# First block of a two-model kernel: when the local attention of the last two token tiles is issued, and which PSUM banks it and the gates use

## The chip, the cores and the metric

The kernel runs on one core of one Trainium2 chip, as one launch. The metric is the device time of an execution in microseconds. Before the change the median of three runs was 1892.68 us, from 1889.23 to 1899.89.

## The reference, cut to what matters

512 tokens of width 1024 pass through a "first block" and then through a second model of two layers. Only the first block's mixer is touched. It projects the normed input and feeds three mixers whose outputs are concatenated and projected again:

```python
proj = h @ w_in
att = swa_sink_alibi(a_q, a_k, a_v, attn_sinks)       # local attention, 4 heads, sinks, ALiBi
ssd = ssd_mixer(s_z, s_xbc, s_dt, ...)                # state space mixer, gated by silu(s_z)
gdn = gdn_mixer(g_qkv, g_z, g_b, g_a, ...)            # gated delta rule, gated by silu(g_z)
mix = jnp.concatenate([att, ssd, gdn], axis=-1) @ w_out
```

The local attention of a token sees its own chunk of 64 tokens and the two before it. It depends on nothing but its queries, keys and values. The delta rule solves a triangular system inside each chunk (this gives u and w), and then carries a 64x64 state per head through the 8 chunks, one after the other. The state space mixer carries a state through the tokens as well.

## The kernel before, in words

All matrices are fp32. A large product is made of three products with operands split into a high and a low part (lines 366 to 368 with the weight stationary, `fm`; lines 380 to 382 with the activation stationary, `tm_k`). Weights come in by DMA on SP's queue, and ScalarE and VectorE split them (lines 345 and 346).

`block1_mix` works on four token tiles of 128 tokens (`t` from 0 to 3). In source order it makes: the norm and the first small projections; the projections with a short convolution (`conv`, `fm_block`); the chunk stage of the delta rule (`chunk_stage`) and a substitution on 16x16 blocks; then the part that the change touches:

- a first loop over the tiles that widens the inverse of the chunk's triangle (lines 808 to 818),
- `ssd(0)`, `swa(0)`, `ssd(1)`, `swa(1)`,
- a second loop over the tiles that gives `gU` and `gW` (lines 823 to 834),
- `ssd(2)`, `swa(2)`,
- a third loop that makes the chunk's transition matrices `At` (lines 838 to 862),
- `ssd(3)`, `swa(3)`,
- the recurrence over 8 chunks (lines 866 to 896): per chunk four matmuls on the state (line 883), a copy of half the result by VectorE (885) and half by ScalarE (886), and the outputs (890, 894),
- the gates: three projections with `k.tm` in 12 groups of 24 matmuls (lines 380 to 382), each group ending in a tanh on ScalarE (447) and a multiply on VectorE (448), which both read the group's PSUM bank,
- norms, transposes into the operand of the output projection (`put_group`, line 357), and the output projection `out_proj`. It takes its eight row blocks in the order `WO1 = (6, 7, 4, 5, 0, 1, 2, 3)`: attention first (6, 7), then the delta rule (4, 5), then the state space mixer.

`swa(t)` does one tile of local attention: for each of two pairs of heads, two matmuls (749), scores with the bias and their maximum (750), softmax on VectorE and ScalarE (753 to 762), four transposes (766, two for tile 0) and a copy (768); then `swa` multiplies with the values (774) and copies the result to `oT` (775). It takes a PSUM bank five times.

PSUM has eight banks. `k.rings` gives names to lists of banks, and `k.ps(name, ...)` hands out the next bank of that list in turn, in source order; whoever gets a bank waits until the last user of it has been read out.

Source order isn't the order on the engines. When the program is built, a planner puts the instructions of each engine in a fixed order: of those that it holds for ready by its own estimates, the one that stands first in the source goes first. So the gates' matmuls, which stand late in the source and need only the normed input and their weights, appear early in the trace between other work. On the chip each engine then keeps that order.

Of the kernel before, what the change touches and what calls it, by code (L numbers as in the profile page):

```python
# [409 lines left out]
def block1_mix(k):  # L410
# [9 lines left out]
    def tile_(shape, name, bufs=1, dt=F32):  # L420
        return (late if name in LATE else P).tile(shape, dt, name=name, bufs=bufs)
# [40 lines left out]
    def bc(ap, n):  # L462

        return ap.unsqueeze(len(ap.shape)).to_broadcast(list(ap.shape) + [n])
# [271 lines left out]
    def swa(t):  # L736
        n = 256 if t else 128
        nk = n // 128
        c0 = t * 128 - (n - 128)
        mx = tile_([128, 4, 4], "amx", 2)  # L740
        pTs = []
        for hp in range(2):
            hs = slice(2 * hp, 2 * hp + 2)
            q = slice(hp * 64, hp * 64 + 64)
            pl = k.ps("s" if t > 1 else "w", [128, 2, 256])
            pr = tile_([128, 2, 256], "cvy", 2)
            for i in range(2):
                h = 2 * hp + i
                E.matmul(pl[:, i, :n], qT[i][q, tok(t)], kT[q, c0:c0 + n], start=True, stop=True)
                V.tensor_tensor_reduce(pr[:, i, :n], pl[:, i, :n], ali[:, h, 256 - n:], scale=1.0,  # L750
                                       scalar=k.row("sinks")[:, h:h + 1], op0=ALU.add, op1=ALU.max,
                                       accum_out=mx[:, 0, h:h + 1])
            V.tensor_scalar(mx[:, 1, hs], mx[:, 0, hs], -1.0, None, op0=ALU.mult)
            V.tensor_tensor(mx[:, 2, hs], k.row("sinks")[:, hs], mx[:, 0, hs], op=ALU.subtract)
            S.activation(mx[:, 2, hs], mx[:, 2, hs], AF.Exp)
            for i in range(2):
                h = 2 * hp + i
                S.activation(pr[:, i, :n], pr[:, i, :n], AF.Exp, bias=mx[:, 1, h:h + 1], accum_out=mx[:, 3, h:h + 1])
            V.tensor_tensor(mx[:, 3, hs], mx[:, 3, hs], mx[:, 2, hs], op=ALU.add)
            V.reciprocal(mx[:, 3, hs], mx[:, 3, hs])  # L760
            for i in range(2):
                V.tensor_scalar(pr[:, i, :n], pr[:, i, :n], mx[:, 3, 2 * hp + i:2 * hp + i + 1], None, op0=ALU.mult)
            pp = k.ps("s" if t > 1 else "w", [128, nk, 2, 128])
            for j in range(nk):
                for i in range(2):
                    E.transpose(pp[:, j, i, :], pr[:, i, j * 128:j * 128 + 128], k.ident)
            pT = tile_([128, 2, 2, 128], "a2w", 2)
            S.copy(pT[:, :nk], pp)
            pTs.append(pT)
        po = k.ps("s" if t > 1 else "w", [128, 2, 128])  # L770
        for hp in range(2):
            q = slice(hp * 64, hp * 64 + 64)
            for j in range(nk):
                E.matmul(po[q], av[:, t - (nk - 1) + j, q], pTs[hp][:, j], start=(j == 0), stop=(j == nk - 1))
        S.copy(oT[:, :, tok(t)], po)

    k.rings(g=(0,1), d=(2, 3, 4), s=(5,6), w=(7,))

    gU = tile_([128, NT, 4, 64], "gU")
    gW = tile_([128, NT, 4, 64], "xt", 3)  # L780
# [2 lines left out]
    def off(t, m):  # L783
        g = tile_([128, 4, 128], "t2k", 5)
        V.tensor_tensor(g.rearrange("p h (c i) -> p h c i", c=2),
                        gA[:, t, :, None, :].to_broadcast([128, 4, 2, 64]),
                        k.c(m).rearrange("p (c i) -> p c i", c=2)[:, None].to_broadcast([128, 4, 2, 64]),
                        op=ALU.mult)
        return g

    def mm4(p, a, b, start=True, stop=True):
        for h in range(4):
            E.matmul(p[:, h, :], a[:, h, :], b(h), start=start and (stop or h == 0), stop=stop and (start or h == 3),
                     skip_group_check=not (start and stop))

    def t2(p):
        o = tile_([128, 4, 128], "t2k", 5)
        S.copy(o, p)
        return o
# [6 lines left out]
    for t in range(NT):  # L806
        d = Dt[t]
# [10 lines left out]
        V.tensor_tensor(d, d, p, op=ALU.add)  # L818
    ssd(0)
    swa(0)  # L820
    ssd(1)
    swa(1)
    for t in range(NT):
        d = Dt[t]
        g2 = off(t, "off32")
        pv = k.ps("d", [128, 4, 128])
        mm4(pv, d, lambda h: rhs[:, t, :, h * 64:h * 64 + 64], stop=False)
        v0 = t2(pv)
        pw = k.ps("d", [128, 4, 128])
        mm4(pw, g2, lambda h: v0[:, h, :])  # L830
        v1 = t2(pw)
        mm4(pv, d, lambda h: v1[:, h, :], start=False)
        V.tensor_tensor(gU[:, t], pv[:, :, 0:64], bc(beta[:, t, :], 64), op=ALU.mult)
        V.tensor_tensor(gW[:, t], pv[:, :, 64:128], bc(nbeta[:, t, :], 64), op=ALU.mult)
    ssd(2)
    swa(2)

    pair = lambda w, q, t, p: w[q, t, 2 * p:2 * p + 2, :].rearrange("p a d -> p (a d)")
    At = []
# [21 lines left out]
                    V.scalar_tensor_tensor(a[r, p, r], k.ident[r, r], sdec[r, t, p, c:c + 1], pa[r, p, r],  # L861
                                           op0=ALU.mult, op1=ALU.add)
    ssd(3)
    swa(3)

    st = [tile_([128, 2, 128], f"st{i}") for i in range(2)]
    for z in st:
# [2 lines left out]
    for t in range(NT):  # L870
        for c in range(2):
# [15 lines left out]
            if c == 0:  # L887
                po = k.ps("d", [128, 4, 64])
# [688 lines left out]
```

## Time and profile before

| | before |
|---|---|
| median of 3 runs | 1892.68 us (1889.23 to 1899.89) |
| profiled execution | 1889.21 us, of which the span from the first to the last instruction is 1887.4 us |
| busy in the span | TensorE 98%, VectorE 56%, ScalarE 39%, GpSimd 7% |
| mean granted clock of TensorE | 0.994 of full |

The profile page has one line per view; the trace can be asked for each engine's instructions in order of time. A row of that timeline gives start, duration, engine, source line, operation, output and inputs, and shape; instructions of one line that follow each other are merged, with their number behind the x. In square brackets stands the idle time of the engine before the row and what ended it. The end of a matmul is modelled and runs into the next one's start, so what a group of matmuls takes is read from its start to the next row's start.

### The profile page before, as it was taken

The page shows a single profiled execution, that of the slowest core. Times are in us where ns is not written, and L with a number is a line of the kernel's source. Part 1 is how long each engine was busy: PE and PEld are TensorE (multiplying, and loading weights), DVE is VectorE, ACT ScalarE, POOL GpSimd, SP SyncE. Part 2 cuts the span into 40 slices and gives each one's busy share as a digit, 9 for nine tenths or more (in the row PEclk, how much of TensorE's full clock was granted, in tenths as well). Part 3 has the DMA queues.
Part 4 walks back from the last instruction along what each step waited for, and adds up shares of the span by engine and source line. Part 5 has one row for each costly group of instructions (what it writes and reads, how often), then busy time and mean ns, then how long its engine had stood idle before and what let it go on. Part 6 is the DMA issues. An engine that isn't in the chain of part 4 may idle for free.

```text
span 1887.4 us, 24192 instructions
## 1 busy us (share of the span) xinstructions
PE 1840.8 (98%) x9467; PEld 1529.9 (81%) x9467; DVE 1066.4 (56%) x1998; ACT 728.2 (39%) x1258; POOL 127.0 (7%) x165
## 2 busy tenths in 40 slices
PE   6999999999999999998999999999999999999998
PEld 6889868888888888865678888888898888888886
DVE  7877776432233357972366643664775476525655
ACT  4533345332332235454644432442433254323432
POOL 1402300000000020121100000000010000000000
PEclk9999999999999999999999999999999999999999
DMA  5221024333333213311043333333333343233321
GB/s 174 79 74 45 23 68 166 102 101 87 103 100 95 74 46 108 107 46 45 22 160 123 93 87 112 92 92 95 96 102 89 101 126 99 90 100 101 95 73 45
DMA packets 49090, 171.50 MB, mean 91 GB/s; under 512 B 5912, under 2 KB 6320, under 8 KB 48720
## 3 DMA queue, kind: packets, MB, share of 16 engines
q1 hardware_dynamic: 44928, 157.90, 27.2%
q10 hardware_dynamic: 3168, 8.25, 1.4%
q0 software_dynamic: 880, 3.82, 0.6%
q8 instruction: 74, 1.21, 0.3%
q14 instruction: 40, 0.33, 0.1%
HBM read 167.81 MB, written 2.13 MB: 90 GB/s over the span
## 4 chain that ended last, share of the span: by engine, by line
PE 50%; ACT 1%; DVE 0%; issue 0%; ACTq 0%; DVEq 0%
PE bank L367 10%; PE bank L366 10%; PE bank L368 10%; PE bank L381 6%; PE bank L382 6%; PE bank L380 6%; PE bank L357 1%; ACT lg L1338 0%; PE bank L1359 0%; ACT pT L1347 0%; ACT whi L345 0%; PE bank L1503 0%; ACT acth L345 0%; PE bank L1366 0%; ACT tsq L984 0%
## 5 line engine op out<-in xcount | busy, mean ns | idle before, releaser
L346 DVE TENSOR_TENSOR wlo<-wraw,whi 128x1024 fp32r<-128x1024 f32 (+3 forms) x295 | 356.3, 1210 | 469.8 <-ACT whi L345 460.6
L366 PE MATMUL bank<-acth,whi 128*128 128x512 f32 (+1 forms) x1528 | 575.7, 379 | 4.7 <-ACT qk L1204 2.9
L367 PE MATMUL bank<-actl,whi 128*128 128x512 f32 (+1 forms) x1528 | 576.1, 378 | 1.9 <-DVE actl L346 1.9
L368 PE MATMUL bank<-acth,wlo 128*128 128x512 f32 (+1 forms) x1528 | 576.0, 377 | 0.0
L345 ACT CAST whi<-wraw 128x1024 fp32r<-128x1024 f32 (+3 forms) x295 | 303.7, 1032 | 590.6 <-PE bank L367 322.2
L366 PEld LDWEIGHTS bank<-acth,whi 128*128 128x128 f32 x1528 | 286.9, 189 | 60.2 <-ACT qk L1204 3.8
L367 PEld LDWEIGHTS bank<-actl,whi 128*128 128x128 f32 x1528 | 288.0, 189 | 54.5 <-DVE actl L346 2.7
L368 PEld LDWEIGHTS bank<-acth,wlo 128*128 128x128 f32 x1528 | 288.1, 189 | 52.2 <-issue 0.3
L380 PE MATMUL bank<-whi,acth 128*128 128x512 f32 (+3 forms) x896 | 317.4, 356 | 4.8 <-ACT v L1478 1.9
L381 PE MATMUL bank<-wlo,acth 128*128 128x512 f32 (+3 forms) x896 | 317.4, 354 | 0.0
L382 PE MATMUL bank<-whi,actl 128*128 128x512 f32 (+3 forms) x896 | 316.0, 354 | 0.0
L380 PEld LDWEIGHTS bank<-whi,acth 128*128 128x128 f32 x896 | 171.0, 191 | 31.2 <-ACT v L1478 2.2
L381 PEld LDWEIGHTS bank<-wlo,acth 128*128 128x128 f32 x896 | 171.4, 191 | 23.5 <-DVE wlo L346 0.5
L382 PEld LDWEIGHTS bank<-whi,actl 128*128 128x128 f32 x896 | 171.1, 191 | 22.7
L1118 DVE SCALAR_TENSOR_TENSOR cv<-bank,fcw,cv 128x510 f32<-128x510 f32 x88 | 65.7, 748 | 2.8
L1117 DVE SCALAR_TENSOR_TENSOR cv<-bank,fcw,cv 128x511 f32<-128x511 f32 x88 | 65.4, 744 | 0.0
L345 ACT CAST acth<-cv 128x512 fp32r<-128x512 f32 x48 | 29.8, 620 | 86.1 <-DVE cv L1135 86.1
L1134 ACT ACTIVATE cv<-cv 128x512 f32<-128x512 f32 x44 | 27.8, 632 | 86.4 <-DVE cv L1118 86.4
L1116 ACT ACTIVATE cv<-bank,fcw 128x512 f32<-128x512 f32 x88 | 59.9, 681 | 0.0
L1131 DVE TENSOR_TENSOR cv<-cv,bank 128x512 f32<-128x512 f32 x22 | 15.1, 688 | 73.8 <-PE bank L368 73.1
L382 PE MATMUL bank<-whi,hid 128*128 128x512 f32 x144 | 56.3, 391 | 0.0
L381 PE MATMUL bank<-wlo,hid 128*128 128x512 f32 x144 | 56.2, 390 | 0.0
(387 smaller groups left out, 1755.2 us busy)
## 6 DMA issues: line engine op xcount, KB each, us to landing
wraw<-in_wf_dram SPq DMA_DIRECT2D x192, 512.0 KB, 3.5
wraw<-in_w_dram SPq DMA_DIRECT2D x63, 512.0 KB, 3.6
wraw<-in_wo_dram SPq DMA_DIRECT2D x24, 512.0 KB, 3.7
gain<-in_gains_dram ACTq DMA_DIRECT2D x12, 512.0 KB, 4.4
wraw<-in_wf_dram SPq DMA_DIRECT2D x12, 256.0 KB, 2.6
xt<-in_x_dram SPq DMA_DIRECT2D x4, 512.0 KB, 5.4
x<-in_x_dram SPq DMA_DIRECT2D x4, 512.0 KB, 5.7
out_dram<-x SPq DMA_DIRECT2D x8, 256.0 KB, 2.0
```

What stands on the lines that cost most here:

```text
L345: self.nc.scalar.copy(hi, src)
L346: (eng or self.nc.vector).tensor_tensor(lo, src, hi.bitcast(F32), op=ALU.subtract)
L366: self.nc.tensor.matmul(ps[:, s], hi[:, k, :], ah, start=(k == 0), stop=False)
L367: self.nc.tensor.matmul(ps[:, s], hi[:, k, :], al, start=False, stop=False)
L368: self.nc.tensor.matmul(ps[:, s], lo[:, k, :], ah, start=False, stop=(k == nk - 1))
L380: self.nc.tensor.matmul(ps, ah, wh, start=first, stop=False)
L381: self.nc.tensor.matmul(ps, ah, wl, start=False, stop=False)
L382: self.nc.tensor.matmul(ps, al, wh, start=False, stop=last)
L1116: S.activation(o, ps, AF.Copy, scale=w(2))
L1117: V.scalar_tensor_tensor(o[:, 1:], ps[:, :T - 1], w(1), o[:, 1:], op0=ALU.mult, op1=ALU.add)
L1118: V.scalar_tensor_tensor(o[:, 2:], ps[:, :T - 2], w(0), o[:, 2:], op0=ALU.mult, op1=ALU.add)
L1134: S.activation(g, g, AF.Silu)
```

## The change

The change does three things. `swa` takes its banks from the ring "w" for every tile (before: "s" for tiles 2 and 3). The ring "w" gets bank 1 beside bank 7, and the ring "g" of the gates keeps bank 0 alone. `swa(2)` moves ahead of the second loop, and `swa(3)` to the place behind `ssd(2)` where `swa(2)` was, ahead of the third loop.

```diff
-            pl = k.ps("s" if t > 1 else "w", [128, 2, 256])
+            pl = k.ps("w", [128, 2, 256])
...
-            pp = k.ps("s" if t > 1 else "w", [128, nk, 2, 128])
+            pp = k.ps("w", [128, nk, 2, 128])
...
-        po = k.ps("s" if t > 1 else "w", [128, 2, 128])
+        po = k.ps("w", [128, 2, 128])
...
-    k.rings(g=(0,1), d=(2, 3, 4), s=(5,6), w=(7,))
+    k.rings(g=(0,), d=(2, 3, 4), s=(5, 6), w=(7, 1))
...
     swa(1)
+    swa(2)
     for t in range(NT):
...
     ssd(2)
-    swa(2)
+    swa(3)
...
     ssd(3)
-    swa(3)
```

## Rows read from the trace of the kernel before

**Rows 1.** Stretches: PE, PEld, DVE, ACT, POOL busy (instructions), granted clock, DMA share, GB/s.

```profile
149.30:266.40 117.10, 116.47 (x929) 101.19 (x927) 87.78 (x223) 46.85 (x121) 33.80 (x28) 1.00 0.11 33
266.40:279.87 13.47, 10.57 (x41) 5.80 (x40) 9.78 (x61) 6.70 (x21) 0.00 (x0) 0.75 0.39 129
215.00:247.00 32.00, 32.00 (x271) 26.62 (x270) 23.52 (x76) 12.36 (x37) 2.55 (x3) 1.00 0.08 21
```

**Rows 2.** Timeline of TensorE at the end of the mixer.

```profile
265.77 0.70 PE L749 MATMUL bank<-cw 64*128 64x256 f32 x2
266.40 0.65 PE L894 MATMUL bank<-st,qtT 128*64 128x128 f32 x4
267.05 0.70 PE L749 MATMUL bank<-cw 64*128 64x256 f32 x2
269.30 1.16 PE L749 MATMUL bank<-cw 64*128 64x256 f32 x2 [1.55 <-DVE amx L750]
...
279.87 0.50 PE L380 MATMUL bank<-whi,acth 128*128 128x512 f32 x1 [0.56 <-ACT acth L345]
```

**Rows 3.** The second stretch, lines 766, 774 and 357 alone: PE, PEld, clock, DMA.

```profile
266.40:279.87 13.47, 2.16 (x8) 1.40 (x8) 0.75 0.39 129
266.40:279.87 13.47, 3.05 (x8) 1.22 (x8) 0.75 0.39 129
266.40:279.87 13.47, 3.14 (x16) 2.04 (x16) 0.75 0.39 129
```

**Rows 4.** Timeline of TensorE: products at full clock, each with its successor.

```profile
237.77 1.08 PE L774 MATMUL bank<-a2w,av 128*64 128x256 f32 x4
238.78 0.37 PE L856 MATMUL bank<-ktil,xt 64*128 64x128 f32 x1
...
317.64 0.39 PE L380 MATMUL bank<-whi,acth 128*128 128x512 f32 x1
317.87 1.03 PE L357 MATMUL bank<-cst,ty 128*128 128x128 f32 x8
318.66 0.48 PE L381 MATMUL bank<-wlo,acth 128*128 128x512 f32 x1
```

**Rows 5.** Timeline of TensorE: last product of swa(2), start and last products of ssd(3).

```profile
244.95 1.08 PE L774 MATMUL bank<-a2w,av 128*64 128x256 f32 x4
245.96 0.44 PE L678 MATMUL bank<-cst,cv 128*128 128x128 f32 x2
...
258.99 1.10 PE L700 MATMUL bank<-xdt,a2k 128*128 128x64 f32 x8
```

**Rows 6.** Timelines of ScalarE and VectorE: last tile of the recurrence, copied and normed.

```profile
267.08 0.37 ACT L896 COPY gU<-bank 128x256 f32<-128x256 f32 x1 [1.81 <-PE bank L894]
275.89 0.43 DVE L918 TENSOR_TENSOR gU<-gU,ro 128x256 f32<-128x256 f32 x1
```

**Rows 7.** Timeline of VectorE: two steps of a reciprocal root in succession.

```profile
252.96 0.17 DVE L405 TENSOR_TENSOR nw<-nw 128x6 f32<-128x6 f32 x1
253.16 0.17 DVE L406 TENSOR_TENSOR nw<-nw,nw 128x6 f32<-128x6 f32 x1
```

**Rows 8.** Timelines of TensorE, VectorE and ScalarE: starts and read-outs of gate groups.

```profile
157.51 0.27 PE L380 MATMUL bank<-whi,acth 128*128 128x192 f32 x1
158.07 0.35 DVE L448 SCALAR_TENSOR_TENSOR gz<-gz,bank 128x192 f32<-128x192 f32 x1 [1.11 <-ACT gz L447]
...
164.98 0.30 PE L380 MATMUL bank<-whi,acth 128*128 128x256 f32 x1
167.05 0.35 DVE L448 SCALAR_TENSOR_TENSOR gz<-gz,bank 128x192 f32<-128x192 f32 x1
...
193.83 0.67 ACT L447 ACTIVATE xt<-bank 128x256 f32<-128x256 f32 x2
195.54 0.74 DVE L448 SCALAR_TENSOR_TENSOR xt<-xt,bank 128x256 f32<-128x256 f32 x2
```

**Rows 9.** A stretch, tile cvy (probabilities of swa(3)) alone: PE, PEld, DVE, ACT.

```profile
260.00:280.00 20.00, 2.16 (x8) 1.40 (x8) 3.07 (x8) 2.36 (x8) 0.83 0.27 89
```

## The prediction

> **What bounds the kernel now.** I read the stretches first. From 149.30 us, where the last convolution's matmuls end, to 266.40, where the recurrence's last four matmuls start, TensorE is busy for 116.47 of 117.10 us at full clock: in this part of the mixer it never waits for more than 0.63 us in all, because the gates' matmuls stand in wherever the chains pause [rows 1]. The next 13.47 us are another matter: VectorE and ScalarE are busy for 9.78 and 6.70 us, and TensorE's granted clock averages 0.75 of full, that is, a part at 1.2 GHz after the engine had idled [rows 1]. The timeline shows why. Behind the recurrence's last products (line 894) TensorE has left only attention (line 749, then 766 and 774), which waits for VectorE, and transposes (line 357), until the output projection starts at 279.87 [rows 2, 3]. After that TensorE is full again for the rest of the kernel (98% of the span). So the change can give time only in these 13.47 us, and can cost time only by opening holes in the 117 us before.
>
> How much is empty there? Of swa(3), two pairs of line 749 are left, at 0.63 us a pair at full clock (265.77 to 266.40): 1.26 [rows 2]. Eight transposes of line 766 and 16 of line 357 [rows 3] go at 0.79 for eight (317.87 to 318.66): 0.79 and 1.58. Eight products of line 774 take two times 1.01 (237.77 to 238.78): 2.02 [rows 3, 4]. With 0.65 for line 894 [rows 2] that is 6.30 us of work, so 7.17 of 13.47 us are empty or lost to the low clock.
>
> Why does attention come last, though it depends on none of this? Its banks. In ring "s" swa(2) stands ahead of ssd(3), and ssd(3) ahead of swa(3). The trace has them in just this order: the last product of swa(2) at 244.95, the first transposes of ssd(3) at 245.96, its last products at 258.99, and only then swa(3) [rows 5].
>
> **The change part by part.** *Attention earlier, in banks of its own.* No instruction is added or taken away on any engine, and none of the moved ones is a DMA; SP and GpSimd get no new entry ahead of theirs. The 4.07 us of attention left at the end (1.26 + 0.79 + 2.02) move into the full stretch and lengthen it by as much, as TensorE has no room there. ssd(3) is free to start when ssd(2) has let go of its banks, without swa(2) in between; this shifts work inside the full stretch and gives gate matmuls back to the recurrence's pauses, with a sum of zero. If all is packed, what stands before the output projection ends at 266.40 + 0.65 + 4.07 + 1.58 = 272.70, and the gain is the 7.17 us.
>
> *What is late next.* The last tile of the delta rule: copied at 267.08, normed at 275.89 [rows 6], because 9.78 us of VectorE's work lie in between, swa(3)'s among it. Alone, this chain is a copy of 0.37 us, a square and a sum (as long as line 918's 0.43 each), about 12 root steps at 0.20 [rows 7], line 918's 0.43, two transposes, a cast and a subtraction (0.4 each): 5.1 us, with hand-overs some 5.6 by estimate. Meanwhile attention's operand is ready, which the output projection takes first: 24 products of 512 columns at 0.23 (317.64 to 317.87) [rows 4]. Their banks are 0 to 3, of which the delta rule's transposes still hold one; so 18 of them, 4.1 us, can run. I charge 1.5 us (5.6 less 4.1); the bounds are 0, if gates are left over too, and 5.6, if nothing fills the gap. At the lower clock the 1.58 us of transposes would cost as much again; I put that inside these bounds. That leaves 5.7 us.
>
> *One bank for the gates.* The cost of a single bank isn't in the trace; it lies between two bounds. Today a group's 24 matmuls start while the last group's bank is still being read. The third group starts at 157.51, its predecessor is read out at 158.42 (158.07 + 0.35): with one bank it starts 0.91 later. The fifth starts at 164.98, and would at 167.40: 2.42 later. The fifth and sixth both wait for ScalarE until 193.83, and for VectorE until 195.54 [rows 8]: with one bank the sixth can't fill TensorE from 170 to 175 as it does now, 24 products of 256 columns or 2.8 us (half of 0.23 each). Lower bound: 0, if other ready work stands in at every boundary. Upper bound: 0.9 and as much again at the boundary after it, 2.4, 2.8, and six later boundaries at 0.9 each, that is 12.3 us. Such a wait stands on TensorE, which keeps its order: where the planner took the bank for free too early, the delta rule's products queue behind the gate's, and VectorE and ScalarE behind these. Before 165 us TensorE has hardly anything but gates, so holes there are real; I take half of the first three (4.2, so 2.1), half of the 2.8 (1.4), and nothing for the later six, where ssd(3) and attention now offer more work. Sum: 3.5 us.
>
> The Trainium skill speaks against this edit: "Perfetto Trace Analysis", section "Optimizing Tensor Performance", under "Matmuls", has independent groups of matmuls rotate through different PSUM banks, so that the read-out of one overlaps the matmuls of the next. The trace agrees in that groups start 0.91 and 2.42 us before the bank ahead of them is read. By that rule the sum would take the upper bound, the rival below.
>
> *Weights.* The output projection's first two weight tiles need a free buffer, and two of the three on hand belong to the gates' last groups. If these end later, loading, casting and splitting begin later; I put this at 0, since the chain of 5.6 us behind the recurrence covers most of such a load, and at 3 us where gates run past the recurrence.
>
> *The sum.* 7.2 less 1.5 less 3.5 is 2.2 us of gain. The profiled execution took 1889.2 (span 1887.4), so it would take 1887.0; the median of the runs shown is 3.5 us above the profiled one, so I forecast 1892.7 - 2.2 = 1890.5.
>
> **The rivals.** *A: all is packed.* The gates' holes are filled by ssd(3) and attention, and the chain at the end by leftover gates and attention's part of the projection. For it: TensorE has 0.63 us of holes in 117 today [rows 1], so the planner finds work. Against it: 2.4 us and more until a bank is read. Gain 7.2, 1885.5; some more if switches between shapes of product get fewer.
>
> *B: the single bank decides (slower).* One mechanism: the read-out of a gate group stands behind all other work on ScalarE and VectorE, as for the groups that waited until 193.83 [rows 8], and the one bank is shut so long that TensorE runs dry. It decides from 5.7 us of holes on, where the gain is used up. With the upper bound, 12.3, the kernel is 6.6 us slower: 1899.3. Against it: between 175 and 193 TensorE was full without any gates.
>
> *C: VectorE becomes the bound.* From 215 to 247 VectorE is busy for 23.52 of 32 us [rows 1]. swa(3) brings it 3.07 us on its probabilities [rows 9] and, by estimate, 1.5 in small steps; ssd(3) brings about as much, so some 9 us come to 8.5 us of room. The third loop, last in line, slips, and the recurrence with it: with 5 us of slip and its pauses filled by gates, 2 us of gain are left at best and 3 lost at worst: 1893.
>
> *D: it doesn't do what it says.* The planner puts swa(3)'s softmax behind the third loop and the recurrence all the same. Then only the single bank counts: 3.5 us lost, 1896. Against it: swa(0) and swa(1), with higher places in the source, ran before the loops behind them.
>
> **How the numbers follow.** Half a per cent, 9.5 us, is what a measurement of this kernel can tell from no change; the three runs shown differ by 0.56%. Forecast 0.50, A 0.20, B 0.12, C 0.11, D 0.07. None of these cases by itself passes 9.5 us; the planner's new order of the whole mixer and the spread of the runs can. I give "faster" 0.10, of which most is A with fewer switches, "slower" 0.10, of which most is B with a late recurrence, and 0.80 to "within 0.5%". The range runs from A less 5 us for such luck, 1880, to B with 2 us of spread, 1901.5.
>
> **What would show it.** Right: swa(3)'s products (line 774) before the recurrence's first (line 883); ssd(3) starting right behind ssd(2); gate groups between the recurrence's steps; the output projection's first product at about 274 to 278 rather than 279.87; TensorE's granted clock near full in the last 10 us before it. Wrong: idle time of TensorE of more than 6 us between 149 and 266 that ends with line 448 (B); VectorE full from 215 on and the recurrence starting later than now (C); line 774 of swa(3) still behind line 894 (D); or a difference that lies behind the output projection's start, for which I have no mechanism.

## The result, and the profile after

The changed kernel is slower: median 1907.37 us of 6 runs (1903.89 to 1910.77), beside 1892.01 for the kernel before in runs on the same chip; ratio 1.0087, 95% interval 1.0064 to 1.0111. The forecast was 1890.5, and the time lies above its range.

Every run lists TensorE's mean granted clock, and the runs lie nearly on lines: within each kernel a run is 1.62 us longer for each 0.001 of mean clock (fit over all kernels; what is left scatters by 0.1 to 1.8 us). The kernel before ran between 0.987 and 0.996 (mean 0.9929 and 1890.6 us over 100 runs), the changed one between 0.989 and 0.993 (0.9905, 1907.2 us). So of 16.5 us between the means, 3.8 go with a lower clock, and 12.7 remain at the same clock. "At the same clock" below always means this: difference of the means to the kernel before, less 1.62 us per 0.001; it is good to about 1 us. (The runs of the kernel before come in five groups of 12 to 28, each on another chip; at the same clock their means differ by less than 0.2 us.) It has two limits. Where a kernel's clock lies outside the range of the kernel before, as in delta_gives_bank, the line is drawn on beyond its runs. And a lower clock that is the edit's own effect is taken out with the rest, so the medians stand beside it.

The profiled execution took 1909.5 us (span 1906.1, clock 0.989). Below are the stretches of the kernel after, with the columns of [rows 1] and cut at the same places in the work: the last convolution product, last four products of line 894, first product of the output projection, table load of the feed-forward part.

```profile
139.50:150.78 11.28, 11.28 (x54) 9.82 (x52) 6.77 (x23) 0.53 (x2) 0.00 (x0) 0.70 0.16 48
150.78:282.64 131.86, 130.74 (x923) 110.27 (x921) 80.60 (x223) 46.23 (x122) 29.87 (x28) 0.92 0.07 21
282.64:290.02 7.38, 4.99 (x38) 4.38 (x37) 5.68 (x27) 5.07 (x14) 0.00 (x0) 1.00 0.00 1
290.02:363.63 73.61, 67.37 (x362) 57.18 (x363) 48.34 (x100) 35.92 (x75) 0.00 (x0) 0.98 0.46 165
```

The first and the last of these have no row in [rows 1]; the kernel before has these:

```profile
139.50:149.30 9.80, 9.80 (x53) 8.45 (x53) 6.29 (x23) 0.47 (x2) 0.00 (x0) 0.83 0.19 55
279.87:344.16 64.29, 63.42 (x352) 54.75 (x353) 40.75 (x65) 33.62 (x69) 0.00 (x0) 1.00 0.41 145
```

The tail did shrink, from 13.47 to 7.38 us. But the full stretch is 14.8 us longer, with 1.12 us without work in it and a mean clock of 0.92, and the projection up to the feed-forward part is 9.3 us longer. Summed over all of TensorE's records from 140 us to the table load (344.2 before, 363.6 after; 1366 products start in that time in both), idle time grew from 4.4 to 9.8 us, and work at the 1.2 GHz level from 9.7 to 30.6 us. Half of such work is lost time, as the steps below show (0.21 us instead of 0.11): 4.9 and 15.3. The rest of the work, counted at the 2.4 GHz level, went from 194.9 to 198.6. That is 5.4 + 10.4 + 3.7 = 19.5 us. (The two profiled runs lie further apart in mean clock, 0.994 and 0.989, than the means, 0.9929 and 0.9905; so the 10.4 are more than the clock costs on the mean.) The 3.7 us are the same products taking longer: from each start to the next, those of line 774 take 1.6 us more in all, those of line 856 and of the gates' line 382 0.9 each. Why is not shown.

**The clock.** One stretch of 20 us in both kernels, before and after:

```profile
156.00:176.00 20.00, 19.73 (x160) 18.49 (x159) 15.93 (x29) 7.86 (x18) 11.71 (x7) 1.00 0.18 54
```

```profile
156.00:176.00 20.00, 19.84 (x81) 17.13 (x80) 12.22 (x33) 5.22 (x18) 7.48 (x6) 0.50 0.01 5
```

TensorE is busy in both, but after it gets through 81 instructions instead of 160. Ahead of the fall stand these rows of TensorE's timeline after:

```profile
151.81 2.38 PE L651 MATMUL bank<-cst,xs 128*128 128x16 f32 x20 [0.53 <-DVE xs L646]
154.12 0.48 PE L749 MATMUL bank<-cw 64*128 64x128 f32 x2
154.53 0.35 PE L380 MATMUL bank<-whi,acth 128*128 128x192 f32 x1
...
155.87 0.41 PE L382 MATMUL bank<-whi,actl 128*128 128x192 f32 x1
```

The first gate group starts at 154.53, where it started at 149.3 before: bank 0, now the gates' only one, still belonged to a late convolution product (in gates_in_bank_1 the group starts at 149.42). In the gap stand a short wait and products of 16 columns; at 155.8 the steps between like products go from 0.11 to 0.21 us. The gap is not what the fall needs: gates_in_bank_1, below, has none and falls as well.

**The end of the gates.** Timeline of TensorE after, around the last groups and the first products of the output projection:

```profile
279.93 0.39 PE L380 MATMUL bank<-whi,acth 128*128 128x256 f32 x1
...
284.77 0.39 PE L380 MATMUL bank<-whi,acth 128*128 128x256 f32 x1 [0.28 <-DVE xt L448]
...
290.02 0.50 PE L380 MATMUL bank<-whi,acth 128*128 128x512 f32 x1 [2.11 <-ACT acth L345]
...
296.15 1.03 PE L357 MATMUL bank<-cst,xs 128*128 128x128 f32 x8
297.75 0.50 PE L380 MATMUL bank<-whi,acth 128*128 128x512 f32 x1 [0.57 <-DVE actl L346]
...
300.55 0.74 PE L357 MATMUL bank<-cst,xs 128*128 128x128 f32 x4 [0.71 <-DVE xs L933]
...
304.42 0.96 PE L380 MATMUL bank<-whi,acth 128*128 128x512 f32 x3 [1.30 <-ACT whi L345]
```

The last gate products end at 287.9, behind the recurrence, and not at 245. Timelines of VectorE and ScalarE: the last group's read-out, the scan's last gating, and what stands before a weight's cast.

```profile
289.85 0.41 DVE L448 SCALAR_TENSOR_TENSOR xt<-xt,bank 128x256 f32<-128x256 f32 x1
...
291.79 0.68 DVE L923 TENSOR_TENSOR xs<-xs,xt 128x512 f32<-128x512 f32 x1
...
301.33 0.59 ACT L345 CAST acth<-bank 128x512 fp32r<-128x512 f32 x1 [0.86 <-PE bank L357]
301.94 1.28 ACT L981 ACT_TABLE_LOAD   x1
303.34 1.03 ACT L345 CAST whi<-wraw 128x1024 fp32r<-128x1024 f32 x1
```

So the transposes of the scan's outputs (`xs`) come from 296.15 to 301, where before they were done at 287. The weights are late too. The projection's eight loads in the timeline of SP's queue, before and then after (a row runs from the first issue to the last of those merged):

```profile
169.14 76.60 SPq L238 DMA_DIRECT2D wraw<-in_wo_dram  x4
268.80 17.20 SPq L238 DMA_DIRECT2D wraw<-in_wo_dram  x4
```

```profile
206.34 83.13 SPq L238 DMA_DIRECT2D wraw<-in_wo_dram  x4
294.17 0.90 SPq L238 DMA_DIRECT2D wraw<-in_wo_dram  x2
305.65 1.47 SPq L238 DMA_DIRECT2D wraw<-in_wo_dram  x2
```

Before, all eight were issued by 286.0; after, the fourth only by 289.5 and the last by 307.1. The hole at 304.42 ends with the weight cast at 303.34. That cast did not wait for its load, as every load issued so far had landed by 299.8: on ScalarE it stands behind the cast of the scan's last operand (301.33), which waits for the late transposes, and a table load of 1.28 us. Last, where the projection ends, before and then after:

```profile
326.00 0.39 PE L382 MATMUL bank<-whi,actl 128*128 128x512 f32 x1
326.35 0.63 PE L366 MATMUL bank<-acth,whi 128*128 128x256 f32 x3
327.60 0.39 PE L367 MATMUL bank<-actl,whi 128*128 128x256 f32 x1 [0.63 <-DVE actl L346]
```

```profile
340.95 0.39 PE L382 MATMUL bank<-whi,actl 128*128 128x512 f32 x1
341.18 1.03 PE L357 MATMUL bank<-cst,ty 128*128 128x128 f32 x8
342.96 0.63 PE L366 MATMUL bank<-acth,whi 128*128 128x256 f32 x3 [0.75 <-ACT acth L345]
346.25 0.38 PE L367 MATMUL bank<-actl,whi 128*128 128x256 f32 x1 [2.66 <-DVE actl L346]
```

Before, the transposes of the second token tile's next norm (`ty`) lie inside the projection, and the feed-forward part follows at once. After, they come behind it, and 3.4 us of holes with them. So the projection loses twice, by late operands (46.1 us from its first to its last product became 50.9) and by closing its tiles late.

### The profile page after: what moved, and what is told of

It reads as the page before. It is cut to its first block, busy times and chain, and to the rows that moved or that the text cites. A ratio compares the mean times of both kernels' runs of the same rounds, so it can differ in the third digit from the quotient of the medians.

```text
span 1906.1 us, 24192 instructions
## 1 busy us (share of the span) xinstructions
PE 1853.5 (97%) x9467; PEld 1540.3 (81%) x9467; DVE 1064.3 (56%) x1998; ACT 727.9 (38%) x1258; POOL 125.4 (7%) x165
## 3 DMA queue, kind: packets, MB, share of 16 engines
HBM read 167.81 MB, written 2.13 MB: 89 GB/s over the span
## 4 chain that ended last, share of the span: by engine, by line
PE 50%; ACT 1%; DVE 1%; issue 0%; DVEq 0%; ACTq 0%
PE bank L367 10%; PE bank L366 10%; PE bank L368 10%; PE bank L381 6%; PE bank L382 6%; PE bank L380 6%; PE bank L357 1%; PE bank L1359 0%; ACT lg L1338 0%; PE bank L1503 0%; ACT whi L345 0%; PE bank L1344 0%; ACT tsq L984 0%; PE bank L1366 0%; DVE wlo L346 0%
## 5 line engine op out<-in xcount | busy, mean ns | idle before, releaser
L1118 DVE SCALAR_TENSOR_TENSOR cv<-bank,fcw,cv 128x510 f32<-128x510 f32 x88 | 65.7, 748 | 2.9
## 6 DMA issues: line engine op xcount, KB each, us to landing
wraw<-in_wf_dram SPq DMA_DIRECT2D x12, 256.0 KB, 2.6
out_dram<-x SPq DMA_DIRECT2D x8, 256.0 KB, 2.0
```

Of the source, the lines that this page charges most:

```text
L1118: V.scalar_tensor_tensor(o[:, 2:], ps[:, :T - 2], w(0), o[:, 2:], op0=ALU.mult, op1=ALU.add)
```

## The experiments

All were timed beside the kernel before. The numbers together:

| run | median us | ratio, 95% interval | mean clock | at the same clock |
|---|---|---|---|---|
| gates_one_bank_alone | 1900.45 | 1.0059 [1.0042, 1.0077] | 0.9904 | +6.2 |
| attention_moved_alone | 1900.27 | 1.0048 [1.0024, 1.0073] | 0.9883 | +1.4 |
| own_ring_in_place | 1904.34 | 1.0067 [1.0043, 1.0091] | 0.9866 | +2.6 |
| moved_old_banks | 1897.25 | 1.0034 [1.0014, 1.0054] | 0.9925 | +5.9 |
| banks_changed_alone | 1908.45 | 1.0106 [1.0083, 1.0129] | 0.9895 | +11.3 |
| moved_bank_1_unused | 1906.81 | 1.0100 [1.0085, 1.0115] | 0.9882 | +8.1 |
| changed kernel | 1907.37 | 1.0087 [1.0064, 1.0111] | 0.9905 | +12.7 |
| changed_banks_renumbered | 1902.50 | 1.0082 [1.0065, 1.0099] | 0.9918 | +10.3 |
| before_banks_renumbered | 1889.60 | 1.0014 [0.9998, 1.0029] | 0.9934 | +0.6 |
| tile_3_in_bank_7 | 1894.01 | 1.0016 [0.9992, 1.0041] | 0.9922 | +2.5 |
| gates_in_bank_1 | 1898.77 | 1.0038 [1.0017, 1.0058] | 0.9905 | +4.6 |
| gate_read_by_one_engine | 1898.38 | 1.0037 [1.0016, 1.0058] | 0.9916 | +5.8 |
| one_reader_bank_1 | 1900.48 | 1.0043 [1.0026, 1.0061] | 0.9945 | +12.7 |
| columns_added | 1902.53 | 1.0060 [1.0040, 1.0080] | 0.9907 | +8.3 |
| ssd_gives_its_bank | 1908.44 | 1.0081 [1.0056, 1.0106] | 0.9902 | +10.5 |
| delta_gives_bank | 1920.65 | 1.0154 [1.0114, 1.0194] | 0.9808 | +11.7 |
| gates_earlier_in_source | 1910.63 | 1.0094 [1.0060, 1.0129] | 0.9875 | +11.3 |
| ungated_scan_changed | 1906.54 | 1.0085 [1.0059, 1.0111] | 0.9898 | +10.6 |
| ungated_scan_before | 1904.87 | 1.0072 [1.0048, 1.0095] | 0.9867 | +4.8 |

### The three edits taken apart

**gates_one_bank_alone**, on the kernel before:

```diff
-    k.rings(g=(0,1), d=(2, 3, 4), s=(5,6), w=(7,))
+    k.rings(g=(0,), d=(2, 3, 4), s=(5,6), w=(7,))
```

> The kernel before with the gates in bank 0 alone and nothing else changed (attention where it was, bank 1 unused). Theory S (the single bank of the gates costs the time): the gates' last group ends after the recurrence, at about 285 us instead of 245, TensorE's clock falls between 150 and 177 us as in the changed kernel, and the kernel is at least as slow as the changed one: 1905 to 1915 us against 1892. Rival M (attention, moved ahead, pushes the delta rule back): the kernel is within 4 us of the one before, and the recurrence starts at about 247 us.

It costs 6.2 us at the same clock. The groups stretch to 271.8 us (244.7 before), and the recurrence starts at 248.1 (247.2 before) but has its last state product at 273.6 (264.4 before), now with gate groups in between. Both theories missed the time: it lies between them.

**attention_moved_alone**, on the changed kernel:

```diff
-    k.rings(g=(0,), d=(2, 3, 4), s=(5, 6), w=(7, 1))
+    k.rings(g=(0, 1), d=(2, 3, 4), s=(5, 6), w=(7,))
```

> The changed kernel with the gates in banks 0 and 1 as before, and attention in bank 7 alone. Theory S: the loss is gone and the gain of the moved attention is seen, 2 to 7 us faster than before: 1885 to 1890. Rival M: the recurrence starts at about 260 us instead of 247, as in the changed kernel, and the kernel stays 10 to 15 us slower than before.

No gain, against theory S: +1.4 at the same clock, and slower still on the median through its low clock. The recurrence starts at 256.0. With one bank the attention is a chain of its own and ends at 285, behind the recurrence.

**own_ring_in_place**, on the kernel before, in all three calls of `swa`:

```diff
-            pl = k.ps("s" if t > 1 else "w", [128, 2, 256])
+            pl = k.ps("w", [128, 2, 256])
```

> The kernel before with attention of all four tiles in ring w (bank 7 alone), in its old places in the source; the gates keep banks 0 and 1. This takes swa(2) and swa(3) out of the queue for the state space mixer's banks without moving them up. Theory O (the move in the source is what delays the delta rule): the recurrence starts within 3 us of 247 us, attention leaves the end, and the kernel is 2 to 6 us faster than before. Rival (any earlier attention delays it, since TensorE has no room): the recurrence starts 4 to 9 us later, and the time is that of the kernel before within 4 us, as much of that as TensorE's clock leaves.

The ring without the move gives no gain either, as the rival said (recurrence at 253.8).

**moved_old_banks**, the reverse of that diff on the changed kernel, with the rings of before:

```diff
-    k.rings(g=(0,), d=(2, 3, 4), s=(5, 6), w=(7, 1))
+    k.rings(g=(0,1), d=(2, 3, 4), s=(5,6), w=(7,))
```

> The changed kernel's order in the source with the rings of the kernel before (gates 0 and 1, attention of tiles 2 and 3 in ring s). Theory O: about the time of attention_moved_alone, 1895 to 1902, recurrence at 254 to 258 us. Rival (the banks, not the order, delay the delta rule): the recurrence starts at about 247 us and the time is that of the kernel before, 1886 to 1892.

The move without new banks costs 5.9 at the same clock. That is the time of theory O, though the recurrence starts at 250.5, earlier than it said. The output projection starts at 269.93, 9.9 us earlier than before, and the feed-forward's table load comes at 348.6, 4.4 us later than before: with attention of tiles 2 and 3 ahead of it in ring "s", `ssd(3)` now ends at 278.3.

**banks_changed_alone**, on the changed kernel, and **moved_bank_1_unused**, the ring line alone:

```diff
     swa(1)
-    swa(2)
...
-    swa(3)
+    swa(2)
...
     ssd(3)
+    swa(3)
```

```diff
-    k.rings(g=(0,), d=(2, 3, 4), s=(5, 6), w=(7, 1))
+    k.rings(g=(0,), d=(2, 3, 4), s=(5, 6), w=(7,))
```

> The changed kernel's banks (gates in bank 0 alone, all attention in banks 7 and 1), with swa(2) and swa(3) back at their places of before. Theory (the one gate bank is the larger half of the cost, the places matter little at the same clock): gates' last product after 265, ratio 1.004 to 1.007, 5 to 8 us above the kernel before at the same mean clock. Rival (the new places are needed for the full loss: attention and the gates together push the recurrence back): ratio under 1.004, under 4 us at the same clock. Third: ratio 1.008 or more, then the places cost nothing at all and the banks everything.

> The changed kernel, but attention has bank 7 alone; bank 1 stays empty in this stage. Theory (attention's second bank lets more of it run ahead, between the gates and the delta rule, and so costs part of the 12.6 us that the change loses at the same mean clock beyond gates alone, 6.1, and moving alone, 1.4): with attention slower the rest adds up to about 7.5 us at the same clock, ratio 1.004 to 1.006. Rival (the loss is the gates' chain with attention ahead of it, with one bank or two): 11 us or more at the same clock, ratio 1.007 or more.

banks_changed_alone has nearly the whole loss: 11.3 of 12.7. TensorE's idle times behind the recurrence are much like those of the changed kernel:

```profile
289.69 0.50 PE L380 MATMUL bank<-whi,acth 128*128 128x512 f32 x1 [2.11 <-ACT acth L345]
297.63 0.50 PE L380 MATMUL bank<-whi,acth 128*128 128x512 f32 x1 [0.77 <-DVE actl L346]
300.23 0.74 PE L357 MATMUL bank<-cst,xs 128*128 128x128 f32 x4 [0.51 <-DVE xs L933]
304.10 1.21 PE L380 MATMUL bank<-whi,acth 128*128 128x512 f32 x4 [1.31 <-ACT whi L345]
```

So the banks are enough for the loss, and the new places add 1.4 to them, which is hardly told from zero. With the old banks the same places cost 5.9: the parts don't add up, and no fixed share belongs to one edit. Gates alone give 6.2, gates with attention moved in one bank 8.1 (its theory had 7.5), and attention's second bank brings it to 10 to 13 (with the renumbered kernel below).

### Is it only a new order?

**changed_banks_renumbered** and **before_banks_renumbered**:

```diff
-    k.rings(g=(0,), d=(2, 3, 4), s=(5, 6), w=(7, 1))
+    k.rings(g=(0,), d=(4, 3, 2), s=(6, 5), w=(1, 7))
```

```diff
-    k.rings(g=(0,1), d=(2, 3, 4), s=(5,6), w=(7,))
+    k.rings(g=(1,0), d=(4, 3, 2), s=(6,5), w=(7,))
```

> The changed kernel with the same number of banks in every ring, taken in another order: d (4, 3, 2), s (6, 5), w (1, 7). No work, place or size is changed. Theory (the loss belongs to the structure of the change): 1903 to 1910, ratio 1.006 to 1.009, within 3 us of the changed kernel at the same clock. Rival (the planner's order is sensitive to anything, and the changed kernel's order is a bad draw): 5 us or more away from it at the same clock, ratio below 1.005 or above 1.011.

> The kernel before with the same banks in every ring, taken in another order: g (1, 0), d (4, 3, 2), s (6, 5). Theory (a new order by itself is worth 2 or 3 us at most): ratio 0.999 to 1.0015. Rival (the kernel before is a good draw among orders, and any new one loses): ratio 1.003 or more, 5 us or more at the same clock; then 5 of the 12.6 us of the change are not its banks or its places but the new draw.

The theory held on both sides: +10.3 and +0.6 (the first median lies 0.5 us under its range). These two reorderings were cheap, which speaks for the change's structure and against a bad draw. They are one draw each: ungated_scan_before, further down, lost 4.8 at the same clock by an edit that only takes a wait away.

### Where does the tail's gain go?

**tile_3_in_bank_7**, on the kernel before, in all three calls:

```diff
-            pl = k.ps("s" if t > 1 else "w", [128, 2, 256])
+            pl = k.ps("s" if t == 2 else "w", [128, 2, 256])
```

> The kernel before with one edit: swa(3) takes its banks from ring w (bank 7) instead of ring s; swa(2) stays in ring s, the gates keep banks 0 and 1, every call keeps its place in the source. Theory (ring s holds swa(3) back, and TensorE has 7 us empty or at the low clock between the recurrence's end and the output projection): swa(3)'s last product (line 774) ends before the recurrence's last, the output projection starts 3 to 5 us earlier than 279.9, the time falls by 3 to 5 us: ratio 0.997 to 0.999. Rival (what stands behind the recurrence is the delta rule's norm chain, and the attention that is taken from there was cover): output projection at 279 to 282, ratio 0.999 to 1.002. Third outcome, as in own_ring_in_place: with one bank swa(3)'s chain is serial and ends late, ratio 1.003 to 1.007.

This is the predicted gain by itself, and it came where the prediction had worked it out: the output projection starts at 272.65 instead of 279.87, more than was expected of this run. It was lost again before the feed-forward part, whose table load starts at 345.2 (344.2 before). The stretch of the projection, with the columns of [rows 1], and rows of its TensorE timeline:

```profile
272.65:345.21 72.56, 67.42 (x356) 56.41 (x357) 45.19 (x93) 34.64 (x72) 0.00 (x0) 0.98 0.44 153
```

```profile
272.65 0.50 PE L380 MATMUL bank<-whi,acth 128*128 128x512 f32 x1 [0.39 <-ACT acth L345]
...
283.85 0.50 PE L380 MATMUL bank<-whi,acth 128*128 128x512 f32 x1 [0.92 <-DVE actl L346]
...
322.57 1.03 PE L357 MATMUL bank<-cst,ty 128*128 128x128 f32 x8
324.36 0.62 PE L366 MATMUL bank<-acth,whi 128*128 128x256 f32 x3 [0.75 <-ACT acth L345]
327.64 0.39 PE L367 MATMUL bank<-actl,whi 128*128 128x256 f32 x1 [2.66 <-DVE actl L346]
```

The projection starts on attention's part while the delta rule's and the scan's are still being normed, and its tiles close late, with the same holes of 0.75 and 2.66 as in the changed kernel. Of the 8.3 us that the stretch is longer than before (72.56 against 64.29), 4.3 are idle time of TensorE (5.14 against 0.87), 1.7 are half of 3.4 us at 1.2 GHz, and the rest is work, four more transposes of line 357 among it (44 against 40). All profiles fall into two kinds by this. Where attention ends last (before, gates_one_bank_alone, attention_moved_alone, own_ring_in_place, moved_bank_1_unused, before_banks_renumbered, ungated_scan_before), first projection product to table load takes 64.2 to 65.7 us. In all others, where attention is done early, it takes 72.0 us or more (73.6 in the changed kernel, 72.6 here). The time counts from the first product, so an early start lengthens it by itself; the division goes with the cause and doesn't prove it.

### The gates' chain, link by link

**gates_in_bank_1**, **gate_read_by_one_engine** (VectorE's step reads ScalarE's result instead of the bank, so the gate's linear factor is left out), and **one_reader_bank_1** (both), on the changed kernel:

```diff
-    k.rings(g=(0,), d=(2, 3, 4), s=(5, 6), w=(7, 1))
+    k.rings(g=(1,), d=(2, 3, 4), s=(5, 6), w=(7, 0))
```

```diff
+    def silu3(out, ps):
+        S.activation(out, ps, AF.Tanh, scale=0.5)
+        V.scalar_tensor_tensor(out, out, 1.0, out, op0=ALU.add, op1=ALU.mult)
```

> The changed kernel with banks 0 and 1 exchanged: gates in bank 1 alone, attention in banks 7 and 0. Bank 0 holds the last convolution's projection until about 151 us, bank 1 is free earlier. Theory C (the low clock of 155.8 to 176.3 us comes from the first gate group starting at 154.5 instead of 149.3 and is a large part of the loss): the first gate group runs at about 149 us, the clock doesn't fall after 150 us, and the kernel is 5 to 10 us faster than the changed one (1897 to 1902). Rival (the read-outs of the one bank set the loss, at any clock): 1904 to 1909, as the changed kernel, with the gates' last group still ending behind the recurrence.

> The changed kernel, but the gates' bank is read by ScalarE alone: the multiply on VectorE takes the tanh twice and doesn't read the bank (the linear factor of the gates is left out; same number and size of instructions). Theory S (how long the single bank stays shut between two groups sets the loss): a boundary shrinks from some 4 us to about 1 to 2 us, the gates' last group ends 10 us or more before the 287.9 us of the changed kernel, and the kernel is 4 to 10 us faster than the changed one: 1897 to 1903. Rival L (the groups are late because they stand last in the source, not because the bank is shut): the last group ends within 4 us of 288, and the time stays within 3 us of the changed kernel's 1907.

> The changed kernel with both edits that each gave back part of the loss: the gates' bank is read by ScalarE alone (the linear factor of the gate is left out), and the gates' one bank is bank 1 (free of the last convolution at once) with attention in banks 7 and 0. Theory (both shorten the one chain of gate groups, by different links): the gains add in part, the first group starts at 149.5, the last gate product comes before 275, output projection at 276 to 281, ratio 1.000 to 1.003. Rival (the recurrence's end at 284 is the bound in both, and the gates are hidden behind it): line 894 still at 283 to 285, output projection at 282, ratio 1.003 to 1.005, no better than either edit alone.

Either edit gives back about 9 us of the median, 7 to 8 at the same clock: the first starts the gates at 149.4, the second ends them at 279.5, 8 us earlier, where theory S had 10 or more. The first has the time that theory C named, and refutes its mechanism: the clock fell all the same, from 154.4 for 20.5 us. Ahead of the fall TensorE does what it does in the kernel before, whose clock stays full there; gate products stand directly in front. First gates_in_bank_1, then the kernel before:

```profile
152.05 0.27 PE L382 MATMUL bank<-whi,actl 128*128 128x192 f32 x1
152.16 2.32 PE L651 MATMUL bank<-cst,xs 128*128 128x16 f32 x20
154.41 0.79 PE L749 MATMUL bank<-cw 64*128 64x128 f32 x2
```

```profile
151.97 0.27 PE L382 MATMUL bank<-whi,actl 128*128 128x192 f32 x1
152.08 2.32 PE L651 MATMUL bank<-cst,xs 128*128 128x16 f32 x20
154.33 0.49 PE L749 MATMUL bank<-cw 64*128 64x128 f32 x2
```

Together the two edits are 7 us faster than the changed kernel on the median, through a clock of 0.992 to 0.997; at the same clock they give back nothing, though the gates start at 149.1, end at 278.8, and the recurrence ends at 278.4. Neither its theory nor its rival had that. The gain was spent in the projection, of 53.7 us from first to last product:

```profile
284.24 0.50 PE L380 MATMUL bank<-whi,acth 128*128 128x512 f32 x1 [0.76 <-DVE actl L346]
289.26 0.65 PE L357 MATMUL bank<-cst,xs 128*128 128x128 f32 x4 [1.09 <-DVE actl L346]
291.31 0.50 PE L380 MATMUL bank<-whi,acth 128*128 128x512 f32 x1 [1.40 <-DVE actl L346]
297.24 1.19 PE L380 MATMUL bank<-whi,acth 128*128 128x512 f32 x4 [1.48 <-ACT whi L345]
```

**gates_earlier_in_source** moves the three gate projections to behind `swa(1)`:

```diff
     swa(1)
+    k.tm([ws.next(4 * 192) for _ in range(2)], act, 192, "g", lambda t, ps: silu2(gz[:, t, 64:256], ps))
...
```

> The changed kernel, banks and all, with the three gate projections moved in the source from behind the recurrence to behind swa(1), ahead of swa(2). Theory (the gate groups end late because they are last in line on ScalarE and VectorE, so that the one bank stays shut): read at once, the groups follow each other quickly, the last product of the 12 groups comes before 250, and the output projection starts at 282 to 286; the recurrence then has no gate products to fill its pauses, which costs 3 to 6 us of them: ratio 1.000 to 1.004. Rival (one bank costs a fill-and-read chain whatever its place in the line): the groups still end behind 270, ratio 1.006 or more.

The groups then end at 252.8 (the theory had "before 250"), and the time doesn't get better. The recurrence starts at 277.7 instead of 260.2, and without gates in its pauses. That the gates end late is therefore not the cause by itself: with the groups put first, the recurrence is late instead.

**columns_added** puts a product of 256 columns behind each of line 651, to fill the thin stretch:

```diff
+        E.matmul(pxw[:, 256:512], act[0][0][:, 0, 0:128], act[0][0][:, 1, 0:256], start=True, stop=True)
```

> The changed kernel with a product of 256 columns behind each of the 16-column products of the second substitution (line 651 of the kernel before): 32 products, 3.8 us of work at full clock, into columns of the same bank that nothing reads. Theory C (the low clock of 155.8 to 176.3 us follows from the thin products and the missing gate groups just ahead, and costs 8 us or more in the runs that have it): the clock stays full after 150 us, and the kernel is 2 to 7 us faster than the changed one in spite of the added work: 1900 to 1905. Rival: the clock falls all the same, or costs nothing, and the kernel is 3 to 5 us slower: 1910 to 1912.

The clock fell all the same, from 153.8 to 170.9 us. Yet the kernel was as fast as theory C said, 4.4 us better than the changed one at the same clock in spite of the added work. What gave that is not shown; it is another sign of what a new order can do.

### A second gate bank from another ring

**ssd_gives_its_bank** and **delta_gives_bank**, on the changed kernel:

```diff
+    k.rings(g=(0, 1), d=(2, 3, 4), s=(5,), w=(7, 6))
```

```diff
+    k.rings(g=(0, 4), d=(2, 3), s=(5, 6), w=(7, 1))
```

> The changed kernel with the gates in banks 0 and 1, attention in banks 7 and 6, and the state space mixer in bank 5 alone. Theory S: faster than before by 0 to 7 us, since the gates have two banks; one bank for the state space mixer delays only that mixer, whose rows the output projection takes last. Rival M: 10 to 15 us slower than before.

> The changed kernel with banks shared out otherwise: gates in two banks (0 and 4), attention in two (7 and 1) as changed, the delta rule's ring d in two banks (2 and 3) instead of three. Theory (most of the loss is the one-bank chain of gate groups, which ends late): the last gate product comes at 246 to 265 instead of 287.6, the output projection starts at 278 to 284 instead of 290.0, ratio 0.999 to 1.003. Rival (the recurrence's own lateness, from attention and ssd(3) put ahead of it, is the loss): recurrence's last products (line 894) still at 280 or later and ratio 1.005 or more. A delta rule slowed by its two banks would show as the start of the recurrence (line 883) later than 262.

Both end the gates early (249.6 and 251.1) and both lose nearly as much as the change. In the first `ssd(3)` ends at 277.7 (260.1 before); in the second the recurrence starts at 277.4, and 47.8 us run at 1.2 GHz from 264.1 on. So neither of these two rings gives a bank away for nothing, and two banks for the gates don't by themselves bring the time back.

### The last consumer of the late gates

**ungated_scan_changed** and **ungated_scan_before**; the scan's outputs are not gated:

```diff
-            V.tensor_tensor(xs[:, t, :], xs[:, t, :], zs[t], op=ALU.mult)
+            V.tensor_tensor(xs[:, t, :], xs[:, t, :], k.row("snw"), op=ALU.mult)
```

> The changed kernel, but the scan's outputs are multiplied by a constant row instead of their gates (the gates are still computed and written, and no longer used for this; the squares go to another scratch tile). Theory (at the same mean clock most of the 12.7 us come from the scan's outputs waiting for the last gates, so that the output projection's operands are late and its four tiles close together): transposes of xs end before 287, no hole over 1 us in the output projection, 6 us or more better than the changed kernel at the same clock, and the difference to ungated_scan_before 6 us or less. Rival (the loss is made earlier, by the bank's chain in front of the recurrence, and the wait for the gates only shows it): 3 us or less better, difference to ungated_scan_before 9 us or more. Third: the weights' buffers, still held by the last gates, take the wait's place; then the holes in the output projection stay and end with a weight's cast.

> The kernel before with the same cut: the scan's outputs are multiplied by a constant row instead of their gates. Theory (here the gates are done at 244.7, long before they are needed): within 2 us of the kernel before at the same clock, ratio 0.998 to 1.001. Rival (the cut lets the scan's norm run earlier and is a gain, or a new order's loss, on its own): 3 us or more either way.

Only 2.1 us came back at the same clock, so my theory for this pair failed. The third outcome is the one seen, weights in the place of the gates. Here, unlike in the changed kernel, the cast did wait for its load (rows of TensorE, then of ScalarE):

```profile
297.06 0.50 PE L380 MATMUL bank<-whi,acth 128*128 128x512 f32 x1 [0.92 <-DVE actl L346]
...
300.86 1.31 PE L380 MATMUL bank<-whi,acth 128*128 128x512 f32 x4 [2.13 <-ACT whi L345]
```

```profile
299.76 1.04 ACT L345 CAST whi<-wraw 128x1024 fp32r<-128x1024 f32 x1 [1.43 <-DMA wraw<-in_wo_dram]
```

The control was not neutral: with a new order, it lost 14.7 us on the means, 10.0 of them by the clock. So the pair, 5.9 us apart at the same clock, bounds nothing more closely.

## Why the prediction was wrong

*Attention earlier.* The mechanism was right: `swa(3)`'s last product came at 258.61, ahead of the recurrence, and the tail shrank. In tile_3_in_bank_7 the projection started at 272.65, where the working had 272.70. That it fits to 0.05 us is luck: the working has 16 transposes, 1.58 us, between the recurrence and the projection, and in the run none stand there (12 of this kind come behind the projection's start), while the recurrence's last products start at 271.61 and not at 266.40 + 4.07 = 270.47.

*What is late next.* This step failed. Charged 1.5 us, bounded at 5.6; measured by the same run, the projection and its end grew by 8.3 (64.3 to 72.6), more than the 7.2 gained. The working looked at the delta rule's operand alone and not at what the projection feeds: 3.4 us of the holes stand behind its last product, where the tiles close late.

*One bank for the gates.* This step failed as well, in size and in form. It was charged 3.5 us, as holes on TensorE; alone it cost 6.2 at the same clock, and with attention's two banks 11.3. But from 150.78 to 282.64 TensorE idles for 1.12 us: other work stood in at nearly every boundary, which the working had as its lower bound of 0. What the single bank does is to spread 12 groups over 133 us (154.5 to 287.9) instead of 96. Between a group's last product and the next one's first lie 0.9 to 7.6 us, 44 in all, and the last groups run behind the recurrence, where the scan's outputs wait for them. (The upper bound adds up to 12.4, not 12.3; nothing hangs on it.)

Either of these two terms, at its measured size, takes away the 2.2 us of forecast gain: 7.2 - 8.3 - 3.5 is -4.6, 7.2 - 1.5 - 6.2 is -0.5. Both together give -7.3. The measured loss at the same clock, 12.7, is more, and which term has the rest stays open.

*Weights.* Charged 0, or 3 us "where gates run past the recurrence". They did, and the loads came late; but the 1.30 at 304.42 is not that wait. There the weight had landed, and its cast stood on ScalarE behind the scan's last operand and a table load. In ungated_scan_changed, with 2.13, it is that wait.

*The clock* was in no term for the stretch before the recurrence. At 156 to 176 it cost 10 us in the profiled run; over the whole kernel, on the means, 3.8. It delays the recurrence: its first state product comes 13.0 us later (247.2 to 260.2), about what half of 20.5 us at 1.2 GHz and the 4.07 us of moved attention make together, 14.3. moved_old_banks, with attention moved and no fall there, has it 3.3 us later (250.5), which fits. That the change is what makes the clock fall is not shown, as gates_in_bank_1 and the last section say.

*The rivals.* B, the single bank, was right in sign and named the right edit; its mark, more than 6 us of idle time ending with line 448, was not seen. Its loss of 6.6 us lies near the 6.2 of gates_one_bank_alone by luck, since it comes from 12.3 us of holes. Of the prediction's signs of being wrong the last one came, a difference behind the start of the output projection, "for which I have no mechanism": 9.3 us. A (a gain), C and D are out: VectorE was less busy than before from 215 to 247 (21.20 of 32 us), and the products moved as written. The recurrence did start later, C's other mark, with VectorE not full. No case of the prediction passes 9.5 us, as the measured loss does; each carried one cost alone.

The rule of the Trainium skill that the prediction weighed ("Perfetto Trace Analysis", section "Optimizing Tensor Performance", "Matmuls": rotate independent groups through banks) was borne out in direction by gates_one_bank_alone, which lost 6.2 us at the same clock. The loss was not seen as TensorE waiting for a read-out: in the changed kernel it idles for 1.12 us from 150.78 to 282.64.

**What stays open.** How the 12.7 us divide inside the edit of the banks is not settled: the links of the gates' chain gave back 7 to 8 us each and nothing together. Edits that should be neutral or cost time moved it by 4 to 5 us (ungated_scan_before, columns_added), so part of any of these differences may be the planner's new order; more orders of one design were not tried. Nor is it shown why attention's second bank costs 2 to 5 us; the early start of the projection that goes with it is one reading.

## What to carry to other kernels

On an engine that is 98% busy, a tail of 7 us can be emptied and bring nothing: follow the released operand to the next stage's end, not to its start. A filler stream (here the gates) is worth what it fills at its time, so ask of a lost bank when the stream then starts and ends, and what waits for its end, beside the wait at each boundary. And take controls that only renumber, better several than one, before a small loss is put down to a design.

## What the runs showed of the hardware

One program spreads over 0.987 to 0.996 of mean granted clock, and its time by 1.6 us per 0.001; this is most of the spread of the runs. A fall to 1.2 GHz that begins between 151 and 164 us is in all eleven profiles with one gate bank (6.8 to 27.3 us long, the middle one 17.1) and in five of nine with two (3.4 to 20.5 us). The products that columns_added put in front of it did not keep it away, nor did gate products directly ahead in gates_in_bank_1, with the order of the kernel before, which did not fall. What would is open.
